# Turning quadrants before the feed-forward operand sums, and moving two key projections one phase later

## The chip, the cores and the metric

The kernel runs on one core of a Trainium2 chip. The metric is the device time of one execution in microseconds (us). Before the change it is 1329.67 us, the median of three runs (1328.03 to 1330.31).

## The reference, cut to what matters

One decoder layer over 1024 tokens of 1024 features, in float32. A combined input projection feeds two groups of heads: eight heads of sparse attention (compressed, selected and windowed keys, gated) and four heads of differential attention (each the difference of two softmax maps over the same values). Their outputs go through one output projection; a residual and a layer norm follow, then a gated feed-forward network (2816 hidden features) and a second residual and norm:

```python
mix = concatenate([o_diff, o_nsa]) @ w_out
x = layer_norm(ALPHA * x + mix, ln1_g, ln1_b)
ffn = (silu(x @ w_gate) * (x @ w_up)) @ w_down
x = layer_norm(ALPHA * x + ffn, ln2_g, ln2_b)
```

## The kernel before, in words

**Precision.** Products that need more than one pass's precision split each operand into a rounded part `hi` and the rest `lo`. `split` (L81) does this: a ScalarE copy makes `hi` (L83), a VectorE or GpSimd subtraction makes `lo` (L85). `mm3` then issues three matmuls, L118, L119 and L120.

**Attention as phases.** The list `phases` (L776) has one entry per pair of sparse heads, and one or two per differential head. An entry names units (one per block of 128 queries), *fillers* (projections for later heads, of 24 matmuls each where keys or queries of 512 tokens are made), how many fillers are due by the middle, and `look`, how many units may have their scores made ahead of the unit that is being finished. A unit has a front (scores L313 and L314, reduction L320 on VectorE, exponentials L334 on ScalarE) and a back (transposes L343 or L353, product with the values L470). `pump` (L808) emits fillers in proportion to the units' costs, and at a priority 2000 later than the units. So a filler runs on TensorE where no unit has work ready, as far as its buffers allow. The scheduler fixes the order of each engine before the run.

**Buffers around the fillers.** A projection accumulates in one of two PSUM buffers `psM` (L62), handed out in turn. Its weights take two `w` tiles and, while they are loaded, a third; there are five. A key projection (`k_fill`, L510) writes its result with L172 and L173 into two slots. Slots 2 and 4 hold the keys of head 1 and then of head 3, slots 0 and 1 those of head 0 and then of head 2. A query projection (`q_fill`, L522) writes with L178 and L179 into two `q` tiles of four, and then needs three transfers `q<-q` (L163), the last of which waits for the first ones. Slots 8 and 9 hold the values of heads 0 and 1 until the last back of head 1, and later the residual rows 0 and 1.

**From attention to the feed-forward network.** The output projection (`out_half`, L578) and first norm (`norm1`, L589) go block by block; `norm1` also stores the normed block to `x1_d` by a transfer of 512 KB. The feed-forward network is computed by a scheme with seven products of quadrants where eight would be plain. For it the normed matrix is cut into quadrants: blocks 0 to 3 and 4 to 7 of tokens, low and high half of the features (`LO`, `HI`). Its operands are the quadrants 11, 21, 22 and the sums T3, T2, T1, T4. Every operand is needed with features in partitions: `x_put` (L866) turns four 128x128 pieces on TensorE into a `psT` bank (L870; three such banks) and splits that bank. `x_sums` (L881) makes the sums of blocks i and i-4 from quadrants with tokens in partitions, and `x_put` turns each of them. In the first round of the feed-forward loop (L1021) the gate's and the up product's first halves stand ahead of `x_sums(7)`, and the operands T1, the last block of 22, and T4 are put between the products that need them.

The functions touched are the `phases` list, `x_put` and `x_sums`, and the loop over blocks that calls `x_put` for 11 and 21. The transposes are written as

```python
for k in range(4):
    nc.tensor.transpose(tp[:, k * P:(k + 1) * P], rows[:, k * P:(k + 1) * P], ident)
```

Of the kernel before, what the change touches and what calls it, by code (L numbers as in the profile page):

```python
# [17 lines left out]
P = 128  # L18
# [21 lines left out]
def layer_kernel(ctx: ExitStack, tc: tile.TileContext, xT, x, w_t, w_vg, w_dv, lam_in, subln,  # L40
# [4 lines left out]
    nc = tc.nc  # L45
# [100 lines left out]
    with ExitStack() as ctx_a:  # L146
# [406 lines left out]
        acc, wo, lnp = [None] * NB, {}, []  # L553
# [8 lines left out]
        def wo_fill(nh):  # L562
            def steps():
                for kp in range(KT // 2):
                    wo[nh, kp] = load_split_here(wo_d[nh, kp], *big_tiles(), l_eng="pool", order=(0, 1))
                yield 0.0
            return steps, 0.0
# [168 lines left out]
        def diff(h, first=0, last=NB):  # L736
            def f():
                if h not in made:
                    made[h] = diff_units(h, qd[h], kd[h], vd[h // 2])
                return made[h][first:last]  # L740
            return f
# [7 lines left out]
        def qdf(h, hf, tiles=w_tiles):  # L749
            return q_fill(8 + 2 * h, hf, qd[h], tiles)  # L750

        def kdf(h, hf):
            return k_fill(9 + 2 * h, ((0, 1), (2, 4))[h % 2], kd[h], (hf,))
# [11 lines left out]
        def held_fill():  # L765

            def steps():
                tc.cur_priority -= FILL_LATER
                finish_held()
                tc.cur_priority += FILL_LATER  # L770
                yield 0.0
            return steps, 0.0

        phases = [  # L776
            (nsa(0), [qf(0, 1), kf(0), qf(1, 0), kf(1)], 1, 0, 1),
            (nsa(1), [qf(1, 1), dvf(0, range(8)), wo_copy(0), qf(2, 0)], 1, 0, 1),
            (nsa(2), [qf(2, 1), kdf(0, 0), wo_copy(1), qf(3, 0), kdf(0, 1)], 1, 0, 1),
            (nsa(3), [qf(3, 1), kdf(1, 0), qdf(0, 0), kdf(1, 1)], 1, 0, 1),  # L780
            (diff(0), [qdf(0, 1), dvf(1, range(4)), qdf(1, 0)], 1, 0, 1),
            (diff(1), [qdf(1, 1), kdf(2, 0), kdf(2, 1), qdf(2, 0)], 1, 0, 1),
            (diff(2, 0, 4), [kdf(3, 0), kdf(3, 1), qdf(3, 0)], 0, 0, 2),
            (diff(3, 0, 4), [qdf(2, 1), dvf(1, range(4, 8))], 0, 0, 2),
            (diff(2, 4), [wo_fill(0), qdf(3, 1), wo_fill(1), held_fill(), out_fill(0, False), out_fill(1, False)], 0, 0, 2),
            (diff(3, 4), [ln_fill((0, 1)), out_fill(2, True), out_fill(3, True)], 0, 0, 2),
        ]
        pending = []
# [63 lines left out]
    LO, HI = slice(0, 512), slice(512, 1024)  # L852
# [10 lines left out]

    X = {n: (x_tile(f"x{n}h"), x_tile(f"x{n}l")) for n in ("11", "21")}

    def x_put(name, i, rows):  # L866

        tp = ps_t()
        for k in range(4):
            nc.tensor.transpose(tp[:, k * P:(k + 1) * P], rows[:, k * P:(k + 1) * P], ident)  # L870
        src = tp.rearrange("p (k t) -> p k t", t=P)
        h, l = X[name]
        n = 4 // len(h)
        cs = slice((i % 4) * P, (i % 4 + 1) * P)
        for j in range(len(h)):
            split(src[:, j * n:(j + 1) * n], h[j][:, :, cs], l[j][:, :, cs])

    def half_tile(n):
        return pb.tile([P, 512], F32, tag=f"half{n}", name=f"half{n}")

    def x_sums(i):  # L881

        b11, b21 = acc[i - 4][:, LO], acc[i - 4][:, HI]
        b12, b22 = acc[i][:, LO], acc[i][:, HI]
        t3, t2 = half_tile(2 * (i % 2)), half_tile(2 * (i % 2) + 1)
        nc.vector.tensor_sub(b11, b12, b11)
        nc.vector.tensor_sub(t3, b22, b12)
        x_put("T3", i, t3)
        nc.vector.tensor_sub(t2, b22, b11)
        x_put("T2", i, t2)  # L890
        nc.gpsimd.tensor_sub(b21, b21, t2)
# [5 lines left out]
    for i in (4, 5):  # L897
        out_start(i)
    for i in range(4):
        x_put("11", i, acc[i][:, LO])  # L900
        x_put("21", i, acc[i][:, HI])
        if i == 2:
            for nh in range(2):
                out_half_now(4, nh, ps_s())
            norm1(4)
# [312 lines left out]
```

## Time and profile before

| | before |
|---|---|
| median of three runs | 1329.67 us (1328.03 to 1330.31) |
| the profiled execution's own time | 1330.62 us |
| its span in the trace | 1328.9 us |
| TensorE (PE) busy | 1301.0 us |
| VectorE (DVE) busy | 914.5 us |
| ScalarE (ACT) busy | 649.7 us |
| GpSimd (POOL) busy | 467.4 us |

The profile is of one execution. Busy time of an engine is the union of its instructions' spans; matmuls are pipelined, so that the span of one overlaps the next and the distance from start to start says what one costs. In the timeline, a bracket behind a row gives the idle time ahead of it and what ended it. Windows give each engine's busy time in a stretch and the granted share of TensorE's clock.

### The profile page before, as it was taken

The numbers are of one execution on the slowest core, as the hardware profiler recorded it, in microseconds if no ns is written. First come the engines' busy times: TensorE is split into PE (matmuls) and PEld (weight loads), VectorE is DVE, ScalarE is ACT, GpSimd is POOL, SyncE is SP. The second block draws the span as 40 slices with busy tenths as digits, with TensorE's granted clock in tenths as the row PEclk, the third lists the DMA queues.
The fourth block names the chain that finished last, engine by engine and source line by source line (L and its number), as shares of the span: only waits on it lengthen the run. The fifth ranks groups of instructions, "written<-read, shape, count | busy, mean of one in ns | idle before, by whom it ended". The sixth has DMA issues, their size and how long they took to land.

```text
span 1328.9 us, 20439 instructions
## 1 busy us (share of the span) xinstructions
PE 1301.0 (98%) x6922; PEld 1106.2 (83%) x6922; DVE 914.5 (69%) x1949; ACT 649.7 (49%) x1398; POOL 467.4 (35%) x504
## 2 busy tenths in 40 slices
PE   9999999999999999999999999999999999999997
PEld 7898998888889878888877888888888888888886
DVE  5536658678798466684687768777767768555588
ACT  5336678676787456652335332332333326533430
POOL 4414354354445336553522232222312232000072
PEclk9999999999999999999999999999999999999999
DMA  9412022130211325532313666655455549868641
GB/s 360 132 27 63 7 59 50 31 80 19 61 25 45 72 59 156 174 113 103 103 64 101 210 203 223 204 168 190 158 192 188 188 152 340 278 200 285 194 171 64
DMA packets 86842, 183.13 MB, mean 138 GB/s; under 512 B 10577, under 2 KB 19153, under 8 KB 86609
## 3 DMA queue, kind: packets, MB, share of 16 engines
q1 hardware_dynamic: 86736, 181.82, 42.4%
q8 instruction: 55, 0.90, 0.3%
q14 instruction: 51, 0.41, 0.1%
HBM read 116.18 MB, written 57.15 MB: 130 GB/s over the span
## 4 chain that ended last, share of the span: by engine, by line
PE 90%; DVE 4%; ACT 2%; DMA 2%; issue 2%; SPq 0%; POOLq 0%; DVEq 0%; POOL 0%; ACTq 0%
PE psM L118 10%; PE psM L120 10%; PE psM L119 10%; PE psT L118 6%; PE psT L119 6%; PE psT L120 6%; PE psS L120 6%; PE psS L118 6%; PE psS L119 6%; PE psT L353 4%; PE psS L313 3%; PE psS L314 3%; PE psO L416 2%; PE psO L470 2%; PE psO L414 2%; PE psO L118 2%
## 5 line engine op out<-in xcount | busy, mean ns | idle before, releaser
L334 ACT ACTIVATE t<-t,m 128x128 f32<-128x128 f32 (+7 forms) x192 | 144.0, 751 | 69.7 <-DVE m L320 66.2
L399 POOL TENSOR_SCALAR t<-t,r,gates 128x640 f32<-128x640 f32 (+7 forms) x128 | 99.6, 784 | 189.3 <-DVE r L393 103.9
L118 PE MATMUL psM<-big,w 128*128 128x512 f32 x304 | 121.9, 401 | 0.5 <-ACT w L83 0.3
L313 PE MATMUL psS<-slot,q 128*128 128x320 f32 (+10 forms) x304 | 113.7, 376 | 8.0 <-DVE m L320 5.3
L119 PE MATMUL psM<-big,w 128*128 128x512 f32 x304 | 119.9, 394 | 0.7 <-POOL big L85 0.7
L120 PE MATMUL psM<-big,w 128*128 128x512 f32 x304 | 119.8, 395 | 0.0
L979 POOL TENSOR_TENSOR half<-half,half 128x512 f32<-128x512 f32 x22 | 33.1, 1502 | 197.6 <-ACT half L978 197.6
L85 DVE TENSOR_TENSOR pt<-psT,pt 128x512 fp32r<-128x512 f32 (+1 forms) x152 | 91.1, 612 | 13.4 <-ACT pt L83 12.8
L314 PE MATMUL psS<-slot,q 128*128 128x320 f32 (+10 forms) x304 | 99.4, 329 | 0.0
L83 ACT CAST pt<-psT 128x512 fp32r<-128x512 f32 (+1 forms) x152 | 77.1, 527 | 32.6 <-PE psT L353 24.0
L83 ACT CAST big<-slot 128x1024 fp32r<-128x1024 f32 (+1 forms) x54 | 54.1, 1018 | 67.5 <-DVE slot L971 58.7
L85 DVE TENSOR_TENSOR op<-op 128x1024 fp32r<-128x1024 f32 x44 | 60.9, 1393 | 35.7 <-ACT op L83 35.3
L353 PE MATMUL psT<-ident,t 128*128 128x128 f32 x528 | 84.0, 274 | 1.4 <-DVE pt L85 0.9
L85 DVE TENSOR_TENSOR big<-slot,big 128x1024 fp32r<-128x1024 f32 (+1 forms) x54 | 63.9, 1191 | 29.2 <-ACT big L83 29.0
L313 PEld LDWEIGHTS psS<-slot,q 128*128 128x128 f32 x304 | 57.4, 189 | 23.1 <-DVE m L320 13.7
L83 ACT CAST op<-op 128x1024 fp32r<-128x1024 f32 x44 | 46.0, 1052 | 60.8 <-DMA op<-t_d 58.4
L320 DVE CUSTOM_DVE_ANT_0 t<-psS,dsel 128x384 f32<-128x384 f32 (+9 forms) x128 | 62.4, 493 | 16.3 <-PE psS L314 15.4
L416 PE MATMUL psO<-pt,slot 128*128 128x256 f32 x264 | 72.9, 299 | 0.3
L983 POOL TENSOR_TENSOR half<-half,half 128x512 f32<-128x512 f32 x22 | 36.5, 1659 | 102.7 <-DVE half L982 102.5
L414 PE MATMUL psO<-pt,slot 128*128 128x256 f32 x264 | 71.0, 288 | 0.1
L118 PEld LDWEIGHTS psM<-big,w 128*128 128x128 f32 x304 | 57.3, 188 | 12.8 <-ACT w L83 1.0
L353 PEld LDWEIGHTS psT<-ident,t 128*128 128x128 f32 x528 | 61.7, 140 | 7.4 <-issue 3.2
(368 smaller groups left out, 3944.9 us busy)
## 6 DMA issues: line engine op xcount, KB each, us to landing
a_d<-slot SPq DMA_DIRECT2D x77, 256.0 KB, 3.0
t_d<-slot SPq DMA_DIRECT2D x77, 256.0 KB, 2.2
q<-q SPq DMA_DIRECT2D x48, 256.0 KB, 2.9
slot<-in_w_up_dram SPq DMA_DIRECT2D x22, 512.0 KB, 3.8
slot<-in_w_down_dram SPq DMA_DIRECT2D x22, 512.0 KB, 3.9
op<-a_d SPq DMA_DIRECT2D x44, 256.0 KB, 4.0
op<-t_d SPq DMA_DIRECT2D x44, 256.0 KB, 4.6
big<-a_d SPq DMA_DIRECT2D x33, 256.0 KB, 3.0
```

What stands on the lines that cost most here:

```text
L83: nc.scalar.copy(hi, src)
L85: eng.tensor_sub(lo, src, hi.bitcast(F32))
L118: nc.tensor.matmul(acc, lhsT=ah, rhs=bh, start=first, stop=False, skip_group_check=more)
L119: nc.tensor.matmul(acc, lhsT=ah, rhs=bl, start=False, stop=False, skip_group_check=more)
L120: nc.tensor.matmul(acc, lhsT=al, rhs=bh, start=False, stop=last, skip_group_check=more)
L313: nc.tensor.matmul(ps[:, :c + part], lhsT=q[0], rhs=k[:, ks], start=True, stop=False)
L314: nc.tensor.matmul(ps[:, :c + part], lhsT=q[1], rhs=k[:, ks], start=False, stop=True)
L334: nc.scalar.activation(t[:, :width], t[:, :width], AF.Exp, bias=m, scale=-1.0, accum_out=r)
L353: nc.tensor.transpose(tp[:rows, n * P:(n + 1) * P], s, ident)
L399: nc.gpsimd.tensor_scalar(t, t, r[:, c:c + 1], gates[:, i, gc:gc + 1], op0=ALU.mult, op1=ALU.mult)
L414: nc.tensor.matmul(po[:, :256], lhsT=v, rhs=pt[:, 0, n * 256:(n + 1) * 256], start=False, stop=False)
L416: nc.tensor.matmul(po[:, :256], lhsT=v, rhs=pt[:, 1, n * 256:(n + 1) * 256], start=False, stop=last)
```

## The change

The quadrants are turned first, and the sums are made of the turned ones. For blocks 0 to 3, the new `x_rows` turns both halves, copies each turned half back over the rows it came from (ScalarE), and splits the bank as before. In `x_sums` the two halves of block i (4 to 7) are turned, 22 is copied back by ScalarE, and the three subtractions and the GpSimd one then work on turned data. `x_put` no longer transposes: for T3, T2, T1, T4 and 22 it splits data that lies in SBUF. Transposes: 28 groups of four before, 16 after.

In the phases, the second half of head 2's keys moves from the phase of head 1 to that of head 2's first blocks; the second half of head 3's keys moves from there to the phase of head 2's last blocks; head 3's first queries go to the front of their phase, with the split weights in slots 8 and 9 in place of `w` tiles; and `look` of head 1's phase is 2.

```diff
+        late_w = lambda: [slot(8), slot(9)]
-            (diff(1), [qdf(1, 1), kdf(2, 0), kdf(2, 1), qdf(2, 0)], 1, 0, 1),
-            (diff(2, 0, 4), [kdf(3, 0), kdf(3, 1), qdf(3, 0)], 0, 0, 2),
+            (diff(1), [qdf(1, 1), kdf(2, 0), qdf(2, 0)], 1, 0, 2),
+            (diff(2, 0, 4), [qdf(3, 0, late_w), kdf(2, 1), kdf(3, 0)], 0, 0, 2),
             (diff(3, 0, 4), [qdf(2, 1), dvf(1, range(4, 8))], 0, 0, 2),
-            (diff(2, 4), [wo_fill(0), qdf(3, 1), wo_fill(1), held_fill(), out_fill(0, False), out_fill(1, False)], 0, 0, 2),
+            (diff(2, 4), [kdf(3, 1), wo_fill(0), qdf(3, 1), wo_fill(1), held_fill(), out_fill(0, False), out_fill(1, False)], 0, 0, 2),
...
-    def x_put(name, i, rows):
+    def by_tile(v):
+        return v.rearrange("p (k t) -> p k t", t=P)
+
+    def turned(rows):
 
         tp = ps_t()
         for k in range(4):
             nc.tensor.transpose(tp[:, k * P:(k + 1) * P], rows[:, k * P:(k + 1) * P], ident)
-        src = tp.rearrange("p (k t) -> p k t", t=P)
+        return tp
+
+    def x_put(name, i, src):
+
+        src = by_tile(src)
...
+    def x_rows(i):
+
+        for name, part in (("11", LO), ("21", HI)):
+            tp = turned(acc[i][:, part])
+            nc.scalar.copy(acc[i][:, part], tp)
+            x_put(name, i, tp)
+
     def x_sums(i):
 
-        b11, b21 = acc[i - 4][:, LO], acc[i - 4][:, HI]
-        b12, b22 = acc[i][:, LO], acc[i][:, HI]
+        b11, b21, b22 = acc[i - 4][:, LO], acc[i - 4][:, HI], acc[i][:, HI]
+        b12t, b22t = turned(acc[i][:, LO]), turned(b22)
         t3, t2 = half_tile(2 * (i % 2)), half_tile(2 * (i % 2) + 1)
-        nc.vector.tensor_sub(b11, b12, b11)
-        nc.vector.tensor_sub(t3, b22, b12)
+        nc.scalar.copy(b22, b22t)
+        nc.vector.tensor_sub(t3, b22, b12t)
         x_put("T3", i, t3)
+        nc.vector.tensor_sub(b11, b12t, b11)
         nc.vector.tensor_sub(t2, b22, b11)
         x_put("T2", i, t2)
         nc.gpsimd.tensor_sub(b21, b21, t2)
...
     for i in range(4):
-        x_put("11", i, acc[i][:, LO])
-        x_put("21", i, acc[i][:, HI])
+        x_rows(i)
```

## Rows read from the trace of the kernel before

**Rows 1.** The page: busy time by engine, and the chain that ended last.

```profile
PE 1301.0 (98%) x6922; PEld 1106.2 (83%) x6922; DVE 914.5 (69%) x1949; ACT 649.7 (49%) x1398; POOL 467.4 (35%) x504
...
PE 90%; DVE 4%; ACT 2%; DMA 2%; issue 2%; SPq 0%; POOLq 0%; DVEq 0%; POOL 0%; ACTq 0%
```

**Rows 2.** Windows by stage: stretch and length, engines' busy time, clock, DMA share, GB/s.

```profile
720.00:1310.00 590.00, 589.99 (x2604) 488.25 (x2603) 415.83 (x491) 218.26 (x285) 143.63 (x93) 1.00 0.60 201
450.00:490.00 40.00, 40.00 (x225) 34.76 (x224) 20.24 (x67) 19.16 (x54) 12.22 (x16) 1.00 0.30 73
...
490.00:500.00 10.00, 6.69 (x38) 4.38 (x37) 9.63 (x26) 7.01 (x17) 6.77 (x7) 1.00 0.16 47
...
520.00:530.00 10.00, 7.88 (x54) 7.67 (x53) 4.17 (x13) 3.30 (x12) 3.21 (x5) 0.83 0.77 217
...
550.00:560.00 10.00, 8.51 (x46) 6.79 (x45) 7.43 (x17) 8.01 (x21) 10.00 (x9) 1.00 0.68 174
560.00:570.00 10.00, 8.73 (x51) 6.35 (x51) 8.73 (x29) 6.41 (x16) 6.07 (x6) 1.00 0.31 109
```

**Rows 3.** All instructions of line L870, by operand: duration min/median/max in ns.

```profile
L870 PE MATMUL psT<-ident,slot x80: 270/272/330, 631.0 to 713.0; 128*128 128x128 f32 x80
...
L870 PE MATMUL psT<-ident,half x32: 271/273/276, 661.7 to 697.1; 128*128 128x128 f32 x32
```

**Rows 4.** TensorE's timeline from 636 us: start, length, line, operation, tiles, count.

```profile
636.26 0.60 PE L870 MATMUL psT<-ident,slot 128*128 128x128 f32 x4
636.62 0.47 PE L118 MATMUL psM<-big,w 128*128 128x512 f32 x1
636.93 0.39 PE L119 MATMUL psM<-big,w 128*128 128x512 f32 x1
637.15 0.39 PE L120 MATMUL psM<-big,w 128*128 128x512 f32 x1
```

**Rows 5.** TensorE's timeline from 680.5 us, ahead of the first feed-forward product.

```profile
680.52 0.60 PE L870 MATMUL psT<-ident,slot 128*128 128x128 f32 x4
681.91 1.33 PE L870 MATMUL psT<-ident,slot 128*128 128x128 f32 x8 [0.79 <-DVE xT3l L85]
683.36 0.50 PE L118 MATMUL psS<-x11h,big 128*128 128x512 f32 x1
...
686.24 0.50 PE L120 MATMUL psS<-x11h,big 128*128 128x512 f32 x1 [1.19 <-DVE big L85]
```

**Rows 6.** Windows from 680 us (columns as in rows 2).

```profile
680.00:690.00 10.00, 7.67 (x40) 5.42 (x38) 9.97 (x16) 6.17 (x11) 1.91 (x3) 1.00 0.22 78
690.00:700.00 10.00, 10.00 (x52) 8.27 (x51) 8.31 (x14) 5.96 (x9) 1.29 (x1) 1.00 0.14 57
```

**Rows 7.** Groups: a ScalarE copy out of PSUM; issues of the x1_d store.

```profile
L962 ACT COPY half<-psS 128x512 f32<-128x512 f32 x1 | 0.6, 589 | 3.1 <-PE psS L120 3.1
...
x_d<-slot SPq DMA_DIRECT2D x8, 512.0 KB, 2.6
```

**Rows 8.** Timelines of GpSimd and VectorE from 709 us.

```profile
709.85 1.84 POOL L979 TENSOR_TENSOR half<-half,half 128x512 f32<-128x512 f32 x1 [13.18 <-ACT half L978]
...
709.86 0.68 DVE L970 TENSOR_TENSOR slot<-slot,slot 128x512 f32<-128x512 f32 x1
710.46 1.78 DVE L971 TENSOR_TENSOR slot<-slot,slot 128x512 f32<-128x512 f32 x1
712.16 0.41 DVE L85 TENSOR_TENSOR w<-psT,w 128x256 fp32r<-128x256 f32 x1
```

**Rows 9.** Timelines of ScalarE and TensorE around the end of head 1.

```profile
495.04 1.04 ACT L172 CAST slot<-psM 64x512 fp32r<-64x512 f32 x2
...
499.34 1.06 ACT L172 CAST slot<-psM 64x512 fp32r<-64x512 f32 x2
...
499.09 1.16 PE L470 MATMUL psO<-slot,pt 128*128 128x128 f32 x8 [1.24 <-ACT pt L346]
...
526.08 0.33 PE L313 MATMUL psS<-slot,q 128*128 128x128 f32 x1 [2.12 <-DMA q<-q]
```

## The prediction

> **What bounds the kernel.** I read the page first. TensorE is busy for 1301.0 us of a span of 1328.9 us and holds 90% of the chain that ended last; VectorE comes next with 914.5 us busy [rows 1]. A busy TensorE is not yet a full one, so I then read windows by stage. From 720 to 1310 us it never rests: 2604 matmuls in 589.99 us, 0.2266 us each [rows 2]. Nothing the change does lies there, but whatever starts that stretch earlier ends the run earlier by as much. The stretches ahead of it differ. In the middle of head 1, 450 to 490 us, TensorE is full as well. At the joins of the differential heads it is not: it rests for 3.31 us from 490 to 500, 2.12 from 520 to 530, 1.49 and 1.27 in the ten-microsecond windows behind 550 [rows 2], 8.2 us in all. The window from 520 also shows a granted clock of 0.83 [rows 2] around that rest. [...] So there are two kinds of places: full stretches, where a removed instruction is worth its issue slot, and joins, where only a removed wait is worth anything.
>
> **Part 1, transposes: what is removed.** The code had 28 groups of four transposes and gets 16, so 48 go: those of 22, T1 and T4. (Those of T3 and T2 are exchanged for the quadrants they are made of, eight per block as before.) A transpose lasts 272 ns by its group [rows 3], but matmuls overlap. The distance between starts tells the price: four transposes take from 636.26 to 636.62, and the matmul behind them costs 0.31 in place of 0.22 or 0.23 [rows 4]; (0.36 + 0.08) / 4 = 0.11 us each. 48 of them are 5.3 us.
>
> Which of these lie on the path? Twelve, those of 22 for blocks 4 to 6, are the two rows from 680.52 to 683.36 [rows 5]. Behind them TensorE waits for an operand from VectorE until 686.24 [rows 5], and VectorE is busy for 9.97 us of those ten [rows 6]. Taking TensorE work out ahead of that wait moves nothing, so these count 0. The other 36, between 697 and 713 us by the end of their group [rows 3], stand among products of a nearly full TensorE, and I count 36 x 0.11 = **4.0 us**. The bounds are 0, if VectorE holds the whole stretch, and 5.3.
>
> **What part 1 adds.** Twelve ScalarE copies of 128x512 out of PSUM, 0.59 us each by a like copy [rows 7]. The eight of blocks 0 to 3 and the ones of blocks 4 and 5 fall where TensorE has output projections to run and hide them; without that cover they would cost 0.59 each. The copy of block 6 stands on ScalarE ahead of the first product's operand, in the stretch without slack, so **0.6 us** against. Each copy overwrites rows that the store to x1_d still reads, 2.6 us from issue to landing [rows 7]. Queued behind the waiting copy on ScalarE are the splits of T3 and T2 and the next norm's activation; VectorE and then TensorE wait for those. For blocks 4 and 5 output projections cover it. For block 7 the first halves of the gate's and the up product cover it: its sums were turned last, at 697.0 us [rows 3], 10 us behind the wait in rows 5; so I count 0. Block 6 has the turning in front of it, about as long as what is left of the store; 0, with 2.6 as the worse bound and, since the scheduler may put the first product's split ahead of it, 1.2 us better (the wait that ends at 686.24 [rows 5]). No DMA is added, and the three PSUM banks held a little longer cost nothing while ScalarE rests for 4 us in ten [rows 6].
>
> A cost that the row count hides: 20 of VectorE's low-part subtractions now read both inputs from SBUF, where one came from PSUM. Beside a GpSimd instruction of 1.84 us, such a one took 1.78 us; alone it took 0.68, and one that reads PSUM took 0.41 at half the size [rows 8]. GpSimd is busy for 1.91 and 1.29 us in the two windows from 680 [rows 6]. I count 0, since VectorE rests for 1.7 us of the ten from 690 [rows 6]; 3.2 us is the worse bound, all of that GpSimd time laid on VectorE. [...]
>
> **Part 2, phases: what is moved.** A projection half is 24 matmuls, 24 x 0.2266 = 5.4 us [rows 2]. None is removed; the count of loads and of q<-q transfers stays. What can change is rest. Before, both halves of head 3's keys are multiplied in head 1's phase, but their write (L172) must wait until head 1's keys in slots 2 and 4 have been scored; it comes at 495.04 and 499.34 [rows 9]. Both psM buffers are held till then, no filler can run, and TensorE rests 3.31 us. After it, only one such half lies there; but head 3's queries, ahead of it, wait for slots 8 and 9, free only after head 1's last back (499.09 [rows 9]). psM is handed out in turn, so this holds fillers as well. I count no gain at that join: bounds -3.3 and +3.3.
>
> The next join is where I expect the gain. Head 3's first queries now come first in their phase, not behind two key halves, so their three transfers, which on SP now go ahead of the loads of head 3's key weights, can land before head 3's first scores. The 2.12 us wait [rows 9] and the 1.7 us of low clock go: **3.8 us**, bounds 0 and 3.8. At the third join, head 3's second key half needs no q tile and can run while the last queries still wait for theirs; the rest from 550 to 570 us, 2.8 us [rows 2], is filled by half: **1.4 us**, bounds 0 and 2.8. Against this I set **1.2 us** for one new wait of the reordered units, of the size of the wait for ScalarE at 499.09 [rows 9]; bounds 0 and 3.3 (twice as many units' tiles in flight, a larger wait at the first join). If the cover of other work is gone, a moved half costs its 5.4 us at its new place. The residual rows 0 and 1 now load into slots 8 and 9 behind both moved halves; the output projection of 10.9 us that uses them last hides that.
>
> **The sum.** Part 1: -4.0 + 0.6 = -3.4. Part 2: -3.8 - 1.4 + 1.2 = -4.0. From the profiled execution's own 1330.62 us this gives **1323.2 us**. That execution stands 0.95 us above the shown median, which is within the runs' spread (1328.03 to 1330.31 without it), so I leave the number there. About 0.2%, 2.7 us, is what a measurement of this kernel can tell from no change: faster means below 1327.0, slower above 1332.3.
>
> **Rivals.**
> (a) *VectorE is the bound from 680 to 712.* It is busy 9.97 and 8.31 of ten [rows 6], and gets the slower subtractions. Part 1 then gains nothing and the copy still costs: 1330.62 + 0.6 - 4.0 = 1327.2, or 1326.6 if the copy hides. Against it: VectorE still rests from 690 [rows 6]. Chance 0.16.
> (b) *Slower: head 1 starves.* Two halves fewer can run inside head 1 (four in place of six, since slots 8 and 9 block the rest). From 490 to 500, without fillers, VectorE was busy 9.63 and TensorE 6.69 [rows 2]: if head 1's units are paced by VectorE and the wait for scores throughout, its phase does not shorten, and 10.9 us of work moves into later stretches. Those absorb 3.8 + 2.8 = 6.6. With 3.3 us of waiting for slots 8 and 9 this is +7.6, less 3.4 from part 1: 1334.8. It decides from where the units cannot run ahead of the removed fillers; VectorE's 20.24 busy of 40 us from 450 [rows 2] speaks against, and so do the two units of look-ahead. Chance 0.10.
> (c) *Every rest goes.* All 8.2 + 1.7 us at the joins and all 5.3 of the transposes: 1330.62 - 15.2 = 1315.4. Against: the dependence on slots 8 and 9. Chance 0.12.
> (d) *A transpose is worth its whole duration*, 0.272 us [rows 3]: 13.1 us, so 1330.62 - 13.1 + 0.6 - 4.0 = 1314.1. The starts [rows 4] speak against it. Chance 0.04. [...]
> That the change does not do what it says I exclude: the calls count 16 groups.
>
> **The numbers.** The forecast has 0.58, with an own range of 1319 to 1328 (its join terms at their bounds). Faster collects 0.54 of it, half of (a), all of (c) and (d): 0.78. The same: 0.12. Slower: 0.10. The range takes in (a) and (c) and leaves out (b) and (d): 1315 to 1330.5.
>
> **What would show it.** L870's or its successor's transposes number 64, spaced 0.11 us. From 679 to 713 us, TensorE's rest grows ahead of the first product by about what 12 transposes took and shrinks behind it. The q<-q wait is gone at the first scores of head 3 and the clock there is 1.00. From the start of the full stretch to the end nothing changes. I am wrong if head 1's phase is as long as before with more rest in it, if TensorE waits for T1 or T4 from VectorE, or if the first product starts more than 2 us later against the end of the output projections.

## The result and the profile after

The changed kernel takes 1338.70 us, the median of six runs (1336.57 to 1339.66), beside 1330.61 us for the kernel before on the same chip (six runs). The ratio is 1.0058, 95% interval 1.0042 to 1.0073: **slower by about 8 us**, where 7.4 us less was forecast. The span in the trace is 1336.8 us.

The page of the changed kernel, engines and chain:

```profile
PE 1298.3 (97%) x6874; PEld 1103.6 (83%) x6874; DVE 908.6 (68%) x1949; ACT 658.2 (49%) x1410; POOL 466.1 (35%) x504
...
PE 88%; DVE 6%; DMA 2%; ACT 2%; issue 1%; POOL 0%; SPq 0%; POOLq 0%; DVEq 0%; ACTq 0%
```

Beside [rows 1]: 48 matmul instructions fewer and 12 ScalarE copies more, as the code says, but VectorE's share of the chain rose from 4% to 6%. The windows of the same stretches as in [rows 2, 6]:

```profile
450.00:490.00 40.00, 37.88 (x236) 31.50 (x235) 29.90 (x116) 26.74 (x82) 17.29 (x24) 1.00 0.28 67
490.00:500.00 10.00, 9.78 (x52) 8.24 (x52) 4.08 (x12) 3.80 (x12) 6.43 (x7) 1.00 0.16 53
520.00:530.00 10.00, 7.48 (x60) 7.04 (x59) 6.57 (x22) 5.57 (x19) 7.30 (x9) 1.00 0.35 79
550.00:560.00 10.00, 10.00 (x56) 8.67 (x55) 5.28 (x15) 6.74 (x15) 9.25 (x8) 1.00 0.70 221
560.00:570.00 10.00, 7.25 (x39) 5.52 (x37) 4.79 (x13) 4.72 (x11) 6.10 (x6) 1.00 0.99 238
570.00:580.00 10.00, 9.12 (x35) 7.68 (x35) 4.46 (x9) 3.24 (x6) 2.86 (x2) 0.66 0.56 146
680.00:690.00 10.00, 9.19 (x41) 7.29 (x39) 10.00 (x16) 5.60 (x11) 4.09 (x2) 1.00 0.01 2
690.00:700.00 10.00, 1.09 (x8) 0.86 (x8) 10.00 (x18) 4.00 (x7) 1.72 (x3) 0.65 0.40 134
700.00:710.00 10.00, 8.73 (x32) 7.17 (x33) 7.97 (x13) 6.39 (x12) 0.66 (x1) 0.67 0.35 128
720.00:1310.00 590.00, 590.00 (x2605) 488.70 (x2603) 412.18 (x480) 220.85 (x288) 143.39 (x93) 1.00 0.61 203
```

The loss is in plain sight from 690 to 700 us: TensorE is busy 1.09 us of ten (10.00 before [rows 6]) while VectorE is busy for all of them. The full stretch behind 720 us holds 2605 matmuls in 590 us, as it held 2604 before [rows 2]. TensorE's timeline of the changed kernel shows the two waits and what follows:

```profile
683.59 0.39 PE L118 MATMUL psS<-x11h,big 128*128 128x512 f32 x1
...
691.59 1.09 PE L874 MATMUL psT<-ident,slot 128*128 128x128 f32 x8 [2.41 <-DVE slot L630]
701.27 1.12 PE L874 MATMUL psT<-ident,slot 128*128 128x128 f32 x4 [8.58 <-DVE slot L622]
702.04 0.78 PE L118 MATMUL psS<-x21h,big 128*128 128x512 f32 x1
702.61 0.63 PE L119 MATMUL psS<-x21l,big 128*128 128x512 f32 x1
703.04 0.63 PE L120 MATMUL psS<-x21h,big 128*128 128x512 f32 x1
```

The first feed-forward product starts at 683.59 us without a wait, 0.2 us from where it started before [rows 5]. Then TensorE stops twice, 11.0 us in all, for the norms of blocks 6 (L630) and 7 (L622); behind that its matmuls start 0.43 us apart, not 0.2266 [rows 2], while the granted clock is 0.65 and 0.67. VectorE in the same stretch:

```profile
684.68 1.28 DVE L85 TENSOR_TENSOR big<-slot,big 128x512 fp32r<-128x512 f32 x2
...
689.39 0.68 DVE L85 TENSOR_TENSOR big<-slot,big 128x512 fp32r<-128x512 f32 x1
689.99 0.41 DVE L85 TENSOR_TENSOR w<-slot,w 128x256 fp32r<-128x256 f32 x1
690.33 1.21 DVE L630 TENSOR_TENSOR slot<-slot,slot 128x1024 f32<-128x1024 f32 x1
...
693.27 0.73 DVE L85 TENSOR_TENSOR w<-slot,w 128x256 fp32r<-128x256 f32 x2
...
697.66 0.67 DVE L85 TENSOR_TENSOR big<-slot,big 128x512 fp32r<-128x512 f32 x1
...
699.46 1.75 DVE L622 SCALAR_TENSOR_TENSOR slot<-slot,mv,slot 128x512 f32<-128x512 f32 x1
...
701.74 0.74 DVE L622 SCALAR_TENSOR_TENSOR slot<-slot,mv,slot 128x512 f32<-128x512 f32 x1
```

It never rests, and the subtractions of L85 out of `slot` into `big` and `w` tiles of 128x512 and 128x256 are the splits of 22, T1 and T4. These operands are needed late, by the gate's fourth and later products, yet ten of their sixteen subtractions start ahead of the end of the norms for which TensorE is waiting. Before, their banks had first to be turned by TensorE, and all but one of them (682.44) came after the norms:

```profile
676.68 1.21 DVE L630 TENSOR_TENSOR slot<-slot,slot 128x1024 f32<-128x1024 f32 x1
...
682.44 0.68 DVE L85 TENSOR_TENSOR big<-psT,big 128x512 fp32r<-128x512 f32 x1
...
687.90 0.74 DVE L622 SCALAR_TENSOR_TENSOR slot<-slot,mv,slot 128x512 f32<-128x512 f32 x1
688.56 0.68 DVE L85 TENSOR_TENSOR big<-psT,big 128x512 fp32r<-128x512 f32 x1
```

Three sums of the gate's weights (L984 to L986, 3.6 us from 683.02 us on) also stand ahead of both norms now; before (L969 to L971) they came behind them, from 689.16 us on. VectorE's instructions are as many as before, 1949.

To find the shares, each trace is cut at two events: the last of the 32 transposes of L488 (the end of head 3's last blocks), and the first feed-forward product. All in us:

| kernel | last L488 | first product | between | from there to the end |
|---|---|---|---|---|
| before | 630.9 | 683.4 | 52.4 | 645.5 |
| after | 640.8 | 683.6 | 42.8 | 653.3 |

So the changed kernel loses its 8 us behind the first product (+7.8), and ahead of it a loss of 9.9 and a gain of 9.6 cancel.

### The profile page after: what moved, and what is told of

The parts are those of the page before. It is cut to its first block, busy times and chain, and to the rows that moved or that the text cites. A ratio compares the mean times of both kernels' runs of the same rounds, so it can differ in the third digit from the quotient of the medians.

```text
span 1336.8 us, 20365 instructions
## 1 busy us (share of the span) xinstructions
PE 1298.3 (97%) x6874; PEld 1103.6 (83%) x6874; DVE 908.6 (68%) x1949; ACT 658.2 (49%) x1410; POOL 466.1 (35%) x504
## 3 DMA queue, kind: packets, MB, share of 16 engines
q1 hardware_dynamic: 86736, 181.82, 42.8%
## 4 chain that ended last, share of the span: by engine, by line
PE 88%; DVE 6%; DMA 2%; ACT 2%; issue 1%; POOL 0%; SPq 0%; POOLq 0%; DVEq 0%; ACTq 0%
PE psM L118 10%; PE psM L120 10%; PE psM L119 10%; PE psT L118 6%; PE psT L119 6%; PE psT L120 6%; PE psS L118 6%; PE psS L119 6%; PE psS L120 6%; PE psT L353 4%; PE psS L313 3%; PE psS L314 3%; PE psO L416 2%; PE psO L414 2%; PE psO L470 2%; PE psO L120 2%
## 5 line engine op out<-in xcount | busy, mean ns | idle before, releaser
L118 PE MATMUL psM<-big,w 128*128 128x512 f32 x288 | 116.3, 404 | 4.6 <-ACT w L83 4.1
L120 PE MATMUL psM<-big,w 128*128 128x512 f32 x288 | 114.3, 398 | 0.3 <-POOL w L85 0.3
L119 PE MATMUL psM<-big,w 128*128 128x512 f32 x288 | 114.5, 398 | 0.0
L85 DVE TENSOR_TENSOR pt<-psT,pt 128x512 fp32r<-128x512 f32 (+1 forms) x152 | 91.1, 612 | 13.4 <-ACT pt L83 12.9
L83 ACT CAST pt<-psT 128x512 fp32r<-128x512 f32 (+1 forms) x152 | 77.1, 527 | 32.6 <-PE psT L353 23.0
L85 DVE TENSOR_TENSOR big<-slot,big 128x1024 fp32r<-128x1024 f32 (+1 forms) x62 | 71.5, 1159 | 29.8 <-ACT big L83 29.6
L83 ACT CAST big<-slot 128x1024 fp32r<-128x1024 f32 (+1 forms) x62 | 59.5, 967 | 64.8 <-DVE slot L986 52.5
L85 DVE TENSOR_TENSOR op<-op 128x1024 fp32r<-128x1024 f32 x44 | 60.0, 1369 | 40.4 <-ACT op L83 37.7
L83 ACT CAST op<-op 128x1024 fp32r<-128x1024 f32 x44 | 45.9, 1051 | 65.4 <-DMA op<-t_d 56.3
L320 DVE CUSTOM_DVE_ANT_0 t<-psS,dsel,m 128x384 f32<-128x384 f32 (+7 forms) x80 | 49.9, 624 | 26.5 <-PE psS L314 25.0
```

The lines of the kernel that those rows point to most:

```text
L83: nc.scalar.copy(hi, src)
L85: eng.tensor_sub(lo, src, hi.bitcast(F32))
L118: nc.tensor.matmul(acc, lhsT=ah, rhs=bh, start=first, stop=False, skip_group_check=more)
L119: nc.tensor.matmul(acc, lhsT=ah, rhs=bl, start=False, stop=False, skip_group_check=more)
L120: nc.tensor.matmul(acc, lhsT=al, rhs=bh, start=False, stop=last, skip_group_check=more)
L320: nc.vector.tensor_tensor_reduce(out=t[:, at:at + part], in0=ps[:, c:c + part], in1=dist[:, at:at + part], scale=slope, scalar=3.0e38 if h ...
```

## The experiments

Theory A: the freed splits take a worse place in the queues of VectorE and ScalarE, whose order the scheduler fixes. Theory B: the chain of each block has become longer, by the copy that waits for the store to `x1_d`. For the phases, theories were formed on the way.

**The parts alone.** E1 has the turned quadrants with the phases list of before; E2 has the new phases list with the quadrants as before.

```diff
 # E1: the change, but
-            (diff(1), [qdf(1, 1), kdf(2, 0), qdf(2, 0)], 1, 0, 2),
+            (diff(1), [qdf(1, 1), kdf(2, 0), kdf(2, 1), qdf(2, 0)], 1, 0, 1),
...
 # E2: before, but
-            (diff(1), [qdf(1, 1), kdf(2, 0), kdf(2, 1), qdf(2, 0)], 1, 0, 1),
+            (diff(1), [qdf(1, 1), kdf(2, 0), qdf(2, 0)], 1, 0, 2),
...
```

What was expected of E1:

> Only the turned quadrants (the second part of the change); the phases are those of before. Both theories of the wait at the first feed-forward products put it in this part: the change is 7.9 us longer than before in the span, TensorE is 3 us late when the output projections end, so this kernel should be about 5 us longer than before (1334 to 1337), with a wait of TensorE of 8 us or more ahead of the transposes of block 7.

What was expected of E2:

> Only the moved key halves (the phases of the change); the quadrants are turned as before. If the parts add, 3 us longer than before (1333 to 1335), with the new wait of TensorE for ScalarE's cast of a mix row (3.6 us, at about 567 us) in it and none at the first feed-forward products. If the parts do not add, no longer than before.

Measured: E1 1337.28 us, ratio 1.0056 [1.0039, 1.0073]; E2 1339.47 us, ratio 1.0071 [1.0053, 1.0089]. Each part loses by itself. E2 is 4 us over what was expected, and its longest wait is not the one expected near 567 us but one of 4.2 us at 684.47 us, ahead of the transposes of the sums. In E1 the expected wait of 8 us is there, but ScalarE ends it and it does not stand at block 7's transposes. TensorE's waits between 676 and 706 us are these two:

```profile
693.78 0.79 PE L118 MATMUL psS<-x21h,big 128*128 128x512 f32 x1 [8.03 <-ACT half L976]
705.60 0.50 PE L118 MATMUL psM<-xT3h,slot 128*128 128x512 f32 x1 [2.54 <-ACT xT3h L83]
```

The first is a wait for ScalarE's copy of the finished first product (L976). ScalarE's own timeline in E1 says why that copy is late:

```profile
689.71 0.62 ACT L83 CAST xT3h<-half 128x512 fp32r<-128x512 f32 x1 [3.56 <-DVE half L901]
690.31 0.62 ACT L83 CAST big<-slot 128x512 fp32r<-128x512 f32 x1
692.11 0.62 ACT L83 CAST xT2h<-half 128x512 fp32r<-128x512 f32 x1 [1.18 <-DVE half L904]
692.63 0.61 ACT L83 CAST slot<-w 128x512 fp32r<-128x512 f32 x1
693.15 0.58 ACT L976 COPY half<-psS 128x512 f32<-128x512 f32 x1
```

It sits behind the casts of block 6's T3 and T2, and these wait for VectorE's sums (L901, L904), which in turn come behind a queue of splits and norms: VectorE has 10.00 and 9.57 us of work in the two windows from 680 us. The wait that ends last carries an ACT name, and its root is VectorE.

**Another order for the freed splits, and no store to wait for.** E3 is E1 with a marker: a copy of a few columns by VectorE into each tile of 22, T1 and T4, from block 7 after its norm, so that their splits can't come before it; the puts of 22 move behind those of T1. E4 is E1 with the stores to `x1_d` of blocks 4 to 7 reading the layer's input, so that no store holds the normed rows (and the second residual of these blocks is not the layer's).

```diff
 # E3: E1, with
+    def hold(name):
+        for h in X[name][0]:
+            nc.vector.tensor_copy(h[:, 0, 0:512:P], acc[7][:, 1020:1024])
...
 # E4: E1, with
-        nc.sync.dma_start(x1_d[i], acc[i])
+        nc.sync.dma_start(x1_d[i], acc[i] if i < 4 else x[i * P:(i + 1) * P, :])
```

What was expected of E3:

> The turned quadrants with the phases of before, and a one-column write of the last normed block into the tiles of 22, T1 and T4, so that their splits cannot be queued on VectorE ahead of the last norms; the puts of 22 stand behind those of T1. Theory A (VectorE's queue: these splits, no longer held back by transposes, went in front of the norms of blocks 6 and 7, and TensorE's in-order queue waits for those norms): the wait of 8 us is gone and the kernel is 2 to 5 us faster than before. Theory B (the chain itself is longer: transposes, a ScalarE copy that waits for the store to x1_d, then the subtractions): the wait stays at 6 us or more and the kernel is slower than before by 3 us or more.

What was expected of E4:

> The turned quadrants with the phases of before; for blocks 4 to 7 the store to x1_d reads the layer's input in DRAM in place of the normed block, so that the copy of 22 waits for no store (the second residual of these blocks is then computed from the input). Theory B: 3 us or more below the kernel with the turned quadrants alone. Theory A: within 1.5 us of it, and the wait ahead of block 7's transposes stays.

Measured: E3 1331.46 us, ratio 1.0016 [1.0005, 1.0027]; E4 1339.03 us, ratio 1.0068 [1.0051, 1.0085]. TensorE's longest waits in E3 between 676 and 706 us:

```profile
689.44 0.80 PE L118 MATMUL psS<-x21h,big 128*128 128x512 f32 x1 [3.45 <-ACT half L979]
700.89 0.50 PE L118 MATMUL psM<-xT3h,slot 128*128 128x512 f32 x1 [3.12 <-ACT slot L83]
```

and in E4:

```profile
695.84 0.80 PE L118 MATMUL psS<-x21h,big 128*128 128x512 f32 x1 [8.01 <-ACT half L976]
```

Order alone is worth 5.8 us (1337.28 to 1331.46). Without the store the wait is the same 8 us, so B falls: in this order the store is not on the path. E3 was expected below the kernel before and was not: the wait for the first product's copy stayed at 3.45 us, and the released splits of T1 and 22 now stood ahead of the third product's operand (`slot`, L83).

**Which half of keys.** E5 moves only head 2's half, with the look-ahead of 2; E6 moves only head 3's. Both also put head 3's first queries in front, with their weights in slots 8 and 9; head 2's half was not moved without that.

```diff
 # E5: before, but
+            (diff(1), [qdf(1, 1), kdf(2, 0), qdf(2, 0)], 1, 0, 2),
+            (diff(2, 0, 4), [qdf(3, 0, late_w), kdf(2, 1), kdf(3, 0), kdf(3, 1)], 0, 0, 2),
...
 # E6: before, but
+            (diff(2, 0, 4), [qdf(3, 0, late_w), kdf(3, 0)], 0, 0, 2),
+            (diff(2, 4), [kdf(3, 1), wo_fill(0),
...
```

What was expected of E5:

> The kernel before with the quadrants as they were; of the two halves of keys only head 2's is moved (out of head 1's phase, with the look-ahead of 2 and the weights of head 3's queries in slots 8 and 9); head 3's second half stays in the phase of head 2's first blocks. Theory C (the loss of the phases comes from taking head 3's half out of the work ahead of the last heads, so that less is left to cover the serial tail at 680): this one costs little, 1328 to 1332, the last transposes of L488 stay near 631 to 633 and no wait over 2 us stands on TensorE at 680. Rival D (the loss comes from head 1's phase, which loses its filler, and from the waits it puts at 520 and 560 to 570): 1334 to 1339, with head 1's phase as late as in the run of both halves.

What was expected of E6:

> The kernel before with the quadrants as they were; of the two halves of keys only head 3's is moved, from the phase of head 2's first blocks to that of its last blocks (the weights of head 3's queries in slots 8 and 9, for which room had to be made). Theory C: nearly the whole loss is here, 1335 to 1340, the last transposes of L488 at 635 to 637 and a wait of some 4 us on TensorE near 680 (4.35 where both halves are moved). Rival D: 1329 to 1332, no such wait.

Measured: E5 1336.26 us, ratio 1.0046 [1.0032, 1.0060]; E6 1330.48 us, ratio 0.9998 [0.9989, 1.0007]. Theory C had the wrong half: the loss is head 2's. But it had the right place. In E5 the last L488 stands at 636.6 us, and TensorE's waits (engine, line, waited for, us in total, times, longest) between 480 and 700 us begin with

```profile
PE psT L871 <- DVE half L888: 4.2, 1, 4.2
PE psS L120 <- DVE big L85: 2.2, 1, 2.2
```

The first ends at 683.67 us, at the transposes of the sums. Counting the matmuls of projections from 440 us to the last L488 in the traces gives 504 before, 514 in E6, 528 in E5 and in the changed kernel. At 0.2266 us [rows 2] the 24 more of E5 are 5.4 us, and the last L488 is 5.6 us later; TensorE's rest over that stretch is the same, 8.05 us for 8.28. In E6 the 10 more, 2.3 us, are paid by 1.8 us less rest (6.50), and its last L488 stands where it stood. From it to the first product E5 takes the same 52.4 us as before: that stretch is the last head's way through output projection, norm and sums, and 26 projection matmuls fewer (164 for 190) are left to run beside it, so TensorE waits.

**Look-ahead and cover.** E10 is E5 with the look-ahead back at 1. E11 is the kernel before with the look-ahead of 2 and nothing else. E13 is E5 with the output projection of block 3 issued behind the attention, to give the tail more cover.

```diff
 # E10: E5, but
-            (diff(1), [qdf(1, 1), kdf(2, 0), qdf(2, 0)], 1, 0, 2),
+            (diff(1), [qdf(1, 1), kdf(2, 0), qdf(2, 0)], 1, 0, 1),
 # E11: before, but
-            (diff(1), [qdf(1, 1), kdf(2, 0), kdf(2, 1), qdf(2, 0)], 1, 0, 1),
+            (diff(1), [qdf(1, 1), kdf(2, 0), kdf(2, 1), qdf(2, 0)], 1, 0, 2),
 # E13: E5, but
-            (diff(3, 4), [ln_fill((0, 1)), out_fill(2, True), out_fill(3, True)], 0, 0, 2),
+            (diff(3, 4), [ln_fill((0, 1)), out_fill(2, True)], 0, 0, 2),
...
+        for _ in out_fill(3, True)[0]():
+            pass
```

What was expected of E10:

> Only head 2's half of keys moved, with the look-ahead of head 1's phase back at 1. Theory G (the loss is made by the cover: 24 more matmuls of the output projections stand ahead of the last transposes of L488, and from these to the first feed-forward product it takes 52.5 us in any order with the old quadrants): the time goes with the start of the last L488. If the look-ahead of 2 is what runs the attention ahead of the fillers, the last L488 falls to 629 to 632 and the time to 1329 to 1332; rival H (that half of the keys is simply gone from the place where it filled, whatever the look-ahead): last L488 at 635 to 637 and 1334 to 1338 as in the run of head 2's half alone (1336.3).

What was expected of E11:

> The kernel before with nothing changed but the look-ahead of head 1's phase, 2 for 1; all keys stay where they were. If the look-ahead is the cause: 1334 to 1338 and the last L488 at 634 to 637. Rival H: 1329 to 1333, last L488 at 629 to 633, with a wait or two moved between 480 and 530.

What was expected of E13:

> Only head 2's half of keys moved, as in the run of 1336.3, but the output projection of block 3 is taken out of the last phase's fillers and issued behind the attention, so that 20 to 48 more of its matmuls are left to cover the tail. Theory G: the last L488 falls by 5 to 10 us (to 627 to 632), the 4.34 us wait at 679 falls to 1 us or less, and the time goes to 1327 to 1332. Rival I (the tail's own chain or its VectorE work has become longer, whatever the cover): the wait near 680 stays over 3 us and the time over 1334; a chain of head 3 that waits by itself without the filler would show as waits over 2 us between 595 and 630.

Measured: E10 1336.83 us, ratio 1.0035 [1.0021, 1.0048]; E11 **1324.99 us, ratio 0.9954 [0.9939, 0.9970]**; E13 1332.36 us, ratio 1.0012 [1.0001, 1.0022]. With head 2's half moved the look-ahead makes no difference (rival H holds). Without the move it gains 6 us, which neither theory had. In E11's timeline the transfer wait of [rows 9] is a quarter of what it was:

```profile
519.94 0.33 PE L313 MATMUL psS<-slot,q 128*128 128x128 f32 x1 [0.51 <-DMA q<-q]
```

and in its windows the joins are fuller, with no drop of the clock:

```profile
490.00:500.00 10.00, 8.84 (x51) 6.11 (x50) 9.49 (x27) 8.79 (x19) 5.27 (x6) 1.00 0.18 54
...
520.00:530.00 10.00, 10.00 (x84) 9.96 (x85) 4.64 (x21) 6.11 (x24) 1.77 (x4) 1.00 0.72 197
...
550.00:560.00 10.00, 8.91 (x43) 6.13 (x43) 8.71 (x26) 6.50 (x18) 8.43 (x9) 1.00 0.41 119
560.00:570.00 10.00, 9.12 (x67) 8.13 (x66) 7.44 (x26) 7.53 (x18) 5.50 (x5) 1.00 0.44 142
```

From 480 to 630 us TensorE is busy 146.33 us in E11 and 141.72 before, 4.6 us more. Before, four transposes L488, five L343 and seven matmuls of 128x256 behind the 2.12 us wait take 3.43 us (526.58 to 530.01 us, in the window at 0.83 [rows 2]); in E11 as many take 1.82 us (0.44, 0.46 and 0.92, from 522.87, 527.76 and 528.22 us). The 4.6 us and this 1.6 make 6.2 of the 6.9 us by which its last L488 comes earlier (624.0).

E13 missed in its mechanism. The projections were to come later; they came earlier still (545 ahead of the last L488, which stood at 638.8 us in a trace that was some 2.5 us late already at 410 us). The wait at the sums shrank to 1.88 us and the time fell by 3.9, though fewer projections were left to run beside the tail, not more (157). That cover decides is thus argued from the equal stretches of E2, E5, E10 (53.0 us) and E11, and E13 doesn't bear it out; why the fixed order puts those 24 projections ahead of head 3's end when head 2's half is moved stays open.

**Mending the order.** E8 is E1 with 22's splits right behind the norm of block 7, and T1's and T4's markers taken from the low part of the gate's third operand. E9 also gives the differences of blocks 4 to 7 other half tiles. E12 is E9 with E6's phases.

```diff
 # E8: E1, with
+        turns.setdefault("o3", o3[1])
...
+            hold("22", acc[7][:, 1020:1024])
...
+            hold("T1", turns["o3"][:, 508:512].bitcast(F32))
...
+            hold("T4", turns["o3"][:, 508:512].bitcast(F32))
 # E9: E8, with
-        t3, t2 = half_tile(2 * (i % 2)), half_tile(2 * (i % 2) + 1)
+        t3, t2 = half_tile((2, 0, 2, 2)[i - 4]), half_tile((3, 1, 3, 3)[i - 4])
```

What was expected of E8:

> The turned quadrants with the phases of before, and the freed splits put in another order: one-column markers hold 22 behind the norm of block 7, and T1 and T4 behind the split of the first third operand, so that the operands of the third products come before T1 and T4. Theory A (it is the place of the freed splits on VectorE and ScalarE alone): of the waits in the held kernel (3.45 for the copy of the first product, 3.12 for the third operand, 0.3) the 3.12 goes; about 3 us under the held kernel's 1331.5, so 1327 to 1330. Rival E (VectorE is full from 674 to 702 whatever the order, so that TensorE only meets another of its operands late): the wait moves to a later product and the time stays 1330 to 1333.

What was expected of E9:

> As the kernel with 22 first, and the differences of blocks 4, 6 and 7 use the half tiles 2 and 3, those of block 5 the tiles 0 and 1, so that ScalarE's copy of the first product (into half tile 0) no longer waits for the split of block 6. Theory A: the 3.45 us wait at 689 falls to 1 us or less as well, 1324 to 1328, below the kernel before (1329.6). Rival E: 1330 to 1333; rival F (ScalarE's queue, not the tile, holds the copy): the wait stays at 3 us and the time is that of the kernel with 22 first.

What was expected of E12:

> The turned quadrants in the order of the markers with the half tiles exchanged (1328.7 alone, ratio 0.9986) together with head 3's half of keys moved (1330.5 alone, ratio 0.9998). If the two do not touch each other: 0.998 to 0.999 of before, about 1328. If the end of the heads leaves less cover for VectorE's work at 680 to 700, which the turned quadrants make the bound there: up to 1332.

Measured: E8 1329.45 us, ratio 0.9988 [0.9978, 0.9998]; E9 1328.74 us, ratio 0.9986 [0.9976, 0.9997]; E12 1330.23 us, ratio 0.9991 [0.9981, 1.0000]. With a good order the turned quadrants gain, though little; between E8 and E9 the runs show no difference, and in E12 nothing is gained on top. In E8 the 3.12 us wait of E3 went and one of 1.82 us came at a later product. In E9 the 3.45 us wait, which E8 still had, went too, so the half tile held the copy, as theory A had it and not rival F: the copy of the first product goes to the half tile in which the turned order keeps block 6's T3 until VectorE has split it (692.68 us in E1, 0.5 us ahead of the copy). But the time did not follow: the wait moved on to the third operand, 3.18 us here and then 1.07, as rival E had it (though the time is under its 1330 us):

```profile
696.83 0.50 PE L118 MATMUL psM<-xT3h,slot 128*128 128x512 f32 x1 [3.18 <-ACT slot L83]
```


**Do the parts add up?** E14 is E9 with the look-ahead of 2; E15 is E1 with the look-ahead of 2.

```diff
 # E14: E9, and E15: E1, but
-            (diff(1), [qdf(1, 1), kdf(2, 0), kdf(2, 1), qdf(2, 0)], 1, 0, 1),
+            (diff(1), [qdf(1, 1), kdf(2, 0), kdf(2, 1), qdf(2, 0)], 1, 0, 2),
```

What was expected of E14:

> The look-ahead of 2 in head 1's phase alone (1325.0, ratio 0.9954) together with the turned quadrants in the order of the markers and the exchanged half tiles (1328.7, ratio 0.9986). If the two parts touch different stretches (waits at 490 to 600, waits at 680 to 705): the ratios multiply, 0.994, some 1322 to 1324. If VectorE's work before the third products is bound to the end of the heads, not to TensorE: both shift together and the sum holds too. Rival J (the fillers' order changes with the quadrants, as in the run of both best, where 1.5 us were lost): 1325 to 1329.

What was expected of E15:

> The turned quadrants without markers (the whole first part of the change) and, of the phases, only the look-ahead of 2, with no keys moved. Theory A with the cover: the wait of 8 us for ScalarE's copy of the first product stays whatever comes before it, so the 7.5 us of the first part are lost from a base 6 us lower: 1331 to 1334, last L488 at 623 to 626. Rival K (the phases' gain and the quadrants' loss are one and the same backlog of VectorE, as the sum of both parts of the change, 8.1 where 7.5 and 9.4 were measured apart, might say): the wait at the first products grows by what is gained earlier, 1336 to 1338.

Measured: E14 **1322.83 us, ratio 0.9942 [0.9928, 0.9955]**, the fastest here, faster than both kernels, and what the product of the ratios gives (0.994); E15 1332.76 us, ratio 1.0013 [1.0004, 1.0022]. E15 is 7.8 us above E11, as E1 is 7.6 above its own before (1329.64): the loss of the unordered splits is fixed, and rival K falls. What is left in E14 between 660 and 710 us starts with

```profile
PE psM L118 <- ACT slot L83: 3.2, 1, 3.2
```

again the third operand's split, with VectorE at 9.77 and 10.00 us in the windows from 680 and 690 us: even in a good order VectorE is the bound there.

The two cuts over the runs put this together:

| kernel | last L488 | first product | between | from there to the end |
|---|---|---|---|---|
| E2, phases only | 637.4 | 690.1 | 52.7 | 645.6 |
| E5, head 2's half | 636.6 | 688.9 | 52.4 | 647.6 |
| E6, head 3's half | 631.0 | 682.6 | 51.7 | 645.3 |
| E10, head 2's half, look-ahead 1 | 636.1 | 689.0 | 53.0 | 646.8 |
| E11, look-ahead | 624.0 | 676.5 | 52.4 | 645.2 |
| E13, projection behind | 638.8 | 688.6 | 49.8 | 644.5 |
| E1, turned only | 630.6 | 679.2 | 48.6 | 654.6 |
| E3, held | 630.0 | 678.6 | 48.6 | 650.5 |
| E4, no store wait | 632.7 | 681.3 | 48.6 | 656.7 |
| E8, 22 first | 629.7 | 678.4 | 48.6 | 649.0 |
| E9, in order | 632.1 | 680.8 | 48.6 | 647.6 |
| E12, in order, head 3's half | 630.5 | 676.8 | 46.4 | 650.9 |
| E14, in order, look-ahead | 624.4 | 673.1 | 48.7 | 647.0 |
| E15, turned, look-ahead | 625.2 | 673.8 | 48.6 | 656.3 |

The phases act mainly on the first column, the quadrants on the last two. (The profiled executions of E1 and E2 lie 1.7 and 2.1 us below their medians, so the columns show less than the whole loss.) That 7.5 and 9.4 us apart, by the ratios, make 8.1 together also follows. With the old quadrants TensorE waits, between the last L488 and the first product, for VectorE's sums before it may turn them; so lost cover shows as a wait. With turned quadrants the transposes need no sums, the stretch between holds no long wait, and it only lasts as long as what is queued: 26 projections fewer are 5.9 us, 48.6 less 5.9 is 42.7, and the changed kernel has 42.8; E12, with 12 fewer, should have 45.9 and has 46.4. The second loss falls away because the first part took its wait out; what the quadrants lose behind the first product stays. E12 shows the limit of it: its shorter stretch comes back behind the first product (650.9 for E9's 647.6), as a wait of 7.0 us for the third operand.

## Why the prediction was wrong

**Part 1, transposes (-4.0).** The price (in the changed kernel four take 0.35 us from 706.98 us, and the matmul behind them 0.31) and the count stood: 48 go. But the gain was looked for in the wrong place. It comes ahead of the first product, where "these count 0" stood: 48.6 us for 52.4, with the 0.79 us wait of [rows 5] and 20 transposes gone from there (8 of these, block 6's, now come behind the first product). The step that failed is the list of what part 1 adds. It priced copies, stores and the slower subtractions, and asked of each which engine's time hides it; it never asked where the twelve groups of splits that no longer wait for TensorE would be put in VectorE's and ScalarE's order. In its terms it is the 0 for block 7 ("the first halves of the gate's and the up product cover it"), where TensorE waited 8.58 us in the changed kernel. Nor did it ask how long a half tile stays taken, which TensorE's turning used to free and VectorE's split frees now (E9). Behind the first product E1 lost 9.1 us, of which 7.0 go when order and half tiles are mended (647.6 for 654.6). Net, the part is worth about -1.9 us at its best (E9), which is half of the term. Rival (a) had named the engine that binds, VectorE from 680 us on, with a chance of 0.16; but it priced this as a gain that is missing, not as a loss.

**"If TensorE waits for T1 or T4 from VectorE"** was named as a sign of being wrong. It did wait for VectorE, but for work queued *behind* T1 and T4. I had read [rows 6] (VectorE busy 9.97 of ten from 680 us) as a reason why nothing is gained there, not as a warning that any instruction that comes earlier there pushes another back.

**The copy of block 6 (+0.6, at worst +2.6).** In ScalarE's timeline of the changed kernel it is

```profile
694.26 0.58 ACT L901 COPY slot<-psT 128x512 f32<-128x512 f32 x1 [3.72 <-DMA x_d<-slot]
```

The store follows the norm that ends at 691.54 us (L630 above), so 2.7 us of this are the store, the stated bound. VectorE had work all the while, so it is not the cause of the stop; in E1's order the copy meets no such wait, and E4 gained nothing without the store. Whether it costs anything on top in the changed kernel's order wasn't tried.

**The slower subtractions (0, at worst 3.2).** They came, and only one of the four delayed instructions is of the kind that was counted. From 675 to 702 us L85 at 675.53, L984 at 683.02, L985 at 687.68 and L622 at 699.46 us took 1.17, 1.73, 1.18 and 1.75 us where 0.68 (L622: 0.74) is usual; before, none there did. Beside two of them GpSimd ran this, in the rows of VectorE and GpSimd:

```profile
675.53 1.17 DVE L85 TENSOR_TENSOR big<-slot,big 128x512 fp32r<-128x512 f32 x1
```

```profile
674.49 1.67 POOL L907 TENSOR_TENSOR slot<-slot,half 128x512 f32<-128x512 f32 x1 [2.90 <-DVE half L905]
...
699.01 1.65 POOL L907 TENSOR_TENSOR slot<-slot,half 128x512 f32<-128x512 f32 x1 [2.86 <-DVE half L905]
```

The four delays are 3.05 us in all, close to the worst bound, on an engine that had no rest to hide it. In the 40 us around the first product E1 has 3.2 us of such delays and E9 3.8, so they are not what separates these two; what they cost in time wasn't tried.

**Part 2, the q<-q wait (-3.8).** That wait went, and the clock from 520 to 530 us is 1.00, as said. The 1.7 us of low clock in this term were the author's estimate, and no run shows them; what the runs show in their place is 1.6 us (3.43 us in the kernel before for what takes 1.82 in E11). The time did not follow: the window rests for 2.52 us where it rested 2.12 [rows 2]. E11 is the run in which the wait falls to 0.51 us and the rest with it, and it earns 6 us, with the look-ahead alone and no key moved.

**The first join (0) and the third (-1.4).** From 490 to 500 us the rest fell from 3.31 to 0.22 us; but 2.12 us of rest appeared from 450 to 490, which was full. Behind 550 us the rest went from 2.76 to 2.75 us, plus 0.88 behind 570.

**The new wait (+1.2, at worst 3.3).** In ScalarE's and in TensorE's timeline of the changed kernel it is

```profile
570.21 0.62 ACT L83 CAST w<-w 128x512 fp32r<-128x512 f32 x1 [3.98 <-DMA w<-mix_d]
```

```profile
570.88 0.79 PE L118 MATMUL psM<-big,w 128*128 128x512 f32 x1 [3.63 <-ACT w L83]
```

a wait for attention output read back for the output projection, with the DMA share at 0.99 from 560 to 570 us; the clock of the next ten is 0.66. The wait is three times the 1.2. Behind it eight matmuls of 128x512, three transposes and eight products L470 take 5.93 us (570.88 to 576.81 us), where the starts of the same kernel elsewhere add up to 3.1: 2.8 us more.

**What part 2 left out.** Even had all rests gone, the balance of fillers would have decided. The prediction took rest away at joins and assumed that what lies behind would shift by the same amount. E5 shows that a moved half also changes which fillers lie ahead of head 3's end, and that the 52 us behind that end don't shrink. Of the 9.9 us by which the changed kernel's last L488 comes later, 5.4 are 24 projections more ahead of it, 2.2 are more rest (10.49 us for 8.28 from 440 us on), and the slower starts behind 570 us (2.8 us more than usual, where the kernel before has 1.6 behind 526 us) make up half of what remains. Rival (b) had the sign ("10.9 us of work moves into later stretches", that don't absorb it) but the opposite mechanism: head 1 did not starve. The fourth of the eight groups of L488's transposes, the last of head 1, came at 501.5 us in the changed kernel and at 526.6 before; the eighth came later.

## What to carry to other kernels

When an instruction is freed from a dependency, ask where a scheduler will now put it in the order of its engine, and who stands behind it there; on an engine that is full, earlier is a cost to someone, and a cheap artificial dependency can be worth more than the work saved. When fillers are moved, count the filler work ahead of and behind the last point from which a serial chain runs to the next stage, since what is left behind that point is the chain's cover. Try each line of a schedule change alone: here the look-ahead, one digit, held all the gain, and the move made with it lost more than that.

## What the runs showed of the hardware

A rest of 8.58 us on TensorE was followed by ten matmuls 0.43 us apart where 0.23 is usual (702.61 to 706.45 us in the changed kernel), with the granted clock at 0.50 in every window of 1 us from 693 to 706 and at 1.00 from 707: some 2 us on top of the rest. Which rests lower the clock the runs don't show. Behind the 2.12 us of the kernel before, the windows of 1 us from 527 to 530 have 0.50, and behind the 3.63 us of the changed kernel those from 571 to 576; behind its 1.76 us (525.63 us) and E11's 0.51 the clock is 1.00. But the changed kernel also rests 2.41 us to 691.59 us, and its clock is 1.00 from 691 to 692 and still 0.95 in the next window, in which the rest of 8.58 us begins.

The four delayed VectorE instructions above, all of whose inputs lie in SBUF (`slot`, `w`, `big`, `mv`), began while a GpSimd instruction ran, and were longer by nearly what GpSimd had left: 1.05, 1.01, 0.50 and 0.49 us longer with 1.19, 1.20, 0.63 and 0.63 left (L984, L622, L985 and L85; ends on GpSimd are rough). Beside the same GpSimd instructions, three with an input in PSUM (L902 at 681.83, L904 at 682.42, L587 at 687.09 us) took 0.67, 0.68 and 0.67 us, no longer than usual. It was not so each time: in E3, L85 at 691.91 us, also with both inputs in SBUF, took 0.68 us in the midst of a GpSimd instruction that itself took 2.23 us (691.51 us, L911) where two like it took 1.67 and 1.64.

The last surprise is in the naming: TensorE's longest waits in E1 and E3 are booked on ScalarE, whose copies take 0.6 us; in E1 ScalarE itself rested for 4.7 of the 8 us (3.56 and 1.18), and the engine that set the wait was VectorE, one step further back.
